# A decoder step on one core: a leeway behind the due time of the merge's and the group norm's matmuls, zero fills moved behind the first rows, and another order of lanes in a triangular solve

## The chip, the cores and the metric

The kernel runs on one core of a Trainium2 chip. The metric is the time of one execution on the device in microseconds. TensorE (PE in the profile) multiplies matrices, VectorE (DVE) and ScalarE (ACT) do elementwise work, GpSimd (POOL) helps with fills and some sums, and SyncE (SP) issues DMA transfers.

## What is computed

One layer of a decoder, for 2048 new tokens of one sequence and four tokens each of eight others, width 1024. Cut to what matters:

```python
h = _rmsnorm(x, norm_g)
p = jnp.einsum('bsd,dn->bsn', h, w_in)            # the large product
xin, bg, cg, zc = _split(p_conv, CONV_SIZES)      # short convolution branch
y_c = bg * conv * jax.nn.silu(zc)
...
def step(S, inp):                                 # RWKV-7 branch, 16 heads of 64
    r_t, k_t, v_t, d_t, kk_t, a_t = inp
    sa = jnp.einsum('bhvk,bhk->bhv', S, -kk_t)
    S = (S * d_t[:, :, None, :] + sa[..., None] * (kk_t * a_t)[:, :, None, :]
         + v_t[..., None] * k_t[:, :, None, :])
    y = jnp.einsum('bhvk,bhk->bhv', S, r_t)
    return S, y
...
mu = jnp.mean(ys, axis=-1, keepdims=True)         # group norm of each head
var = jnp.mean(jnp.square(ys - mu), axis=-1, keepdims=True)
yn = ((ys - mu) * lax.rsqrt(var + GN_EPS)).reshape(b, s, D_RWKV) * ln_w + ln_b
...
m = jax.nn.sigmoid(gc) * (y_c @ w_out_c) + jax.nn.sigmoid(gr) * (y_r @ w_out_r)
y = _rmsnorm(x + m @ w_o, final_g)
```

## The kernel before

**Main stream and side work.** TensorE executes its instructions in the order in which the program issues them. Most of them are the main stream: the projection of the normalised rows, held in two halves `XH` and `XL`, with the weights, also in two halves (`whl`), block by block of 128 columns, into PSUM tiles named `ip`. The 2048 tokens are taken in four sets of 512; the last set carries the 32 sample tokens too.

Between the matmuls of the main stream lies the recurrent branch, as side work. For each set and each of eight pairs of heads (32 pairs in all) it is cut into generators, called sides: `rwkv_keys` (kind "keys"), `rwkv_solve` ("solve"), `rwkv_merge` ("merge", L1260), `rwkv_load` ("load"), `rwkv_chain` ("chain", L1368), for the samples `rwkv_sequences` ("samp"), and `rwkv_out` ("out", L1483; for the very last pair it has the kind "close"). The recurrence is taken in chunks of 64 tokens. A chunk needs the inverse of a 64 by 64 triangular matrix; `rwkv_solve` inverts its 32 by 32 diagonal blocks row by row on VectorE, `rwkv_merge` puts the inverse together, and `rwkv_chain` then goes through the chunks with two kinds of matmul per chunk on the path, `pb<-UB,Xbd` and `pb<-SV,BKt`, behind `pa<-S,AR`.

**The planner.** While the program is built, a clock (`Clock`, L134 for `add`) follows every instruction with a cost from `cost` and notes when each result should be there. After every matmul of the main stream `drive` (L557) offers each live side a turn. `Side.run` takes a step of a side when its share of the window is due, when its VectorE backlog is small enough (not asked of the kinds listed in `URGENT`, among them chain, merge and load), and when the clock of TensorE has reached `self.due`. That due time is set by the step before: the side yields the operands that its next step needs, and L533 asks the clock when they are ready.

```python
self.due = clock.ready(aps) if aps else 0.0
```

So a product of a side is put into TensorE's order at the first main matmul behind the planned end of its operands. If an operand is late on the chip, TensorE waits with everything behind it. Each side may only begin when those named in its `after` list have ended: the chain of a pair behind the merge and the load of that pair and the "out" of the pair before (`run_pair`, L1781). When the ring of eight `tmp` buffers is empty, `push` (L543) forces steps of samples, keys and out without asking for the due time. The order of VectorE and ScalarE is that of the planned starts (`clock.begun`, near the end of the first phase); only the kinds listed in `LOOSE` are left out of it.

**The solve and the merge.** `rwkv_solve` turns `Mc` (32 rows of eight chunks) with one VectorE transpose of 1024 elements into `Mi`, so that a lane of 32 belongs to a chunk c and one of four column groups e; `X` starts as the identity `X0` in the same lane order. After 31 rows of updates a second transpose brings `X` back as `Xo` (it takes the buffer `Mi`, and stands in the trace as `Mi<-X`). `rwkv_merge` copies it on ScalarE in four copies to the block matrix `Xbd` (`Xbd<-Mi` in the trace), transposes a part on VectorE into `T11` (`Mc<-Xbd`), and yields; then come 16 small products `pt<-Mc,GM` and 16 `pt<-Mc,Mo`, two ScalarE copies, a yield, 32 products `pt<-Xbd,X`, copies, and a last yield. In the last set more products with the samples' part of `Xbd` follow, one step each. The planner's price of a VectorE transpose is 145 + 1.12 n ns up to 256 elements and 145 + 1.86 n ns above (L303); that of a ScalarE copy from SBUF is 190 + 0.84 n ns, and 190 + 1.9 n where the innermost stride of its input is over 1.

**The group norm.** `rwkv_out` subtracts the mean, squares on ScalarE, sums, takes the root (GpSimd's power and three VectorE steps), scales `Yc`, transposes it on TensorE (`pt<-ident,Yc`) and applies weights and gates. It yields operands four times.

**The start.** Two tiles of 128 rows of x are loaded into `GM`, their squares are summed on ScalarE, and `rsq_steps` (L595) gives the root: a VectorE `tensor_scalar`, the power on GpSimd, two products, a second `tensor_scalar` (`nw<-nw`) and a product (`rstd`). Then VectorE scales the first tile (`GM<-GM,rstd`, noted as `setup["scaled"][0]`) and ScalarE the second; TensorE transposes both in 16 pieces (`ip<-ident,GM`); VectorE, ScalarE and GpSimd split them into `XH` and `XL` (`to_cols`, L764); then the main stream begins. `zero_rest` (L1754) fills, on GpSimd, the buffers `UP`, `BK`, `AR`, `Xbd`, `UB`, `SV` and the eight states `S` with zeros. It stands later in the program, but its kind is in `LOOSE` and it depends on nothing, so the order of GpSimd has it wherever that engine has room.

After the last pair a second phase of some 590 us multiplies the branches with the output weights; the change does not touch it.

Every operation of the profile carries L264, the line of the helper that records it (`r = f(*a, **k)`), and every load and store of SyncE's queue L337.

Of the kernel before, what the change touches and what calls it, by code (L numbers as in the profile page):

```python
# [7 lines left out]
F32 = mybir.dt.float32  # L8
# [3 lines left out]
ALU = mybir.AluOpType  # L12
# [4 lines left out]
P = 128  # L17
# [4 lines left out]
NCH = 8  # L22
# [154 lines left out]


ROOM = {"samp": 2}


class Ring:
# [162 lines left out]
def hybrid_kernel(tc, x_prompt, x_sample, state_conv, state_shift, state_rwkv, norm_g, w_in, conv_w,  # L345
# [4 lines left out]
    clock = Clock()  # L350
    V, A, G, T = (Traced(e, n, clock) for e, n in ((nc.vector, "DVE"), (nc.scalar, "ACT"), (nc.gpsimd, "POOL"), (nc.tensor, "PE")))
# [15 lines left out]
    TW = NT + 64  # L367
# [37 lines left out]

    order = []
    raws, parts_, lows = {}, {}, []
    setup = {"casts": [], "lows": [], "scaled": {}}
    state = {"use": 0, "dma": 0, "split": 0}

    def w_advance(dma, split, load):
# [91 lines left out]
    class Side:  # L503
# [15 lines left out]
        def run(self, upto, force=False, once=False):  # L519
            if any(not x.ended for x in self.after) or upto < self.f0:  # L520
                return
            goal = float("inf") if once else weight[self.kind] * (upto - self.f0) / max(1e-9, self.f1 - self.f0) if upto < self.f1 else float("inf")
            while self.given < goal and self.f0 <= upto and (force or len(tmp.open) >= ROOM.get(self.kind, 0) and max(self.due, pt_free(self.banks)) <= clock.t["PE"] and (
                    self.kind in URGENT or clock.load("DVE") < BACKLOG)):
                try:
                    clock.kind = self.kind
                    x = next(self.g)
                    clock.kind = None
                    x, aps, self.banks = (x + ((), 0)[len(x) - 1:]) if isinstance(x, tuple) else (x, (), 0)
                    if x == "free":  # L530
                        self.f0, x = self.gate, 0.0
                    self.given += x
                    self.due = clock.ready(aps) if aps else 0.0  # L533
                    if once:
                        return
                except StopIteration:
                    clock.kind = None
                    weight[self.kind] = self.given
                    self.ended = True
                    live.remove(self)  # L540
                    break
# [68 lines left out]
    tmp = Ring(ph1.enter_context(tc.tile_pool(name="tmp", bufs=1)), [P, NT + 64], 8, clock)  # L610
# [62 lines left out]
    for hr in range(2):  # L673
        for q in range(2):
            sl = mask_p[hr * 64:(hr + 1) * 64, q]
            G.affine_select(out=sl, in_=sl, pattern=[[1, 64]], compare_op=ALU.is_gt if q == 0 else ALU.is_ge,
                            fill=0.0, base=0, channel_multiplier=-1)
# [3 lines left out]
    for hr in range(2):  # L681
        sl = seqm[hr * 64:(hr + 1) * 64, :]
# [9 lines left out]
                        in1=seqm.unsqueeze(2).broadcast_to([P, NS, SL]), op=ALU.mult)  # L692

    X0 = con.tile([P, 8, 32], F32, name="X0")
    xo0 = tmp.tile([P, TW], F32, name="tmp")[:, 0:256].rearrange("p (a b c) -> p a b c", b=4, c=8)
    G.memset(xo0, 1.0)
    for g in range(4):
        sl = xo0[g * 32:(g + 1) * 32]
        G.affine_select(out=sl, in_=sl, pattern=[[-4, 8], [-1, 4], [0, 8]], compare_op=ALU.is_equal, fill=0.0,
                        base=0, channel_multiplier=1)  # L700
    V.transpose(X0.rearrange("p a b -> p (a b)"), xo0.rearrange("p a b c -> p (a b c)"))
    tmp.free(xo0)

    rst = con.tile([P, NT], BF16, name="rst")
# [496 lines left out]
    col = [slice(32 * b, 32 * b + 32) for _ in range(2) for b in range(2)]  # L1201
    blk = [(slice(64 * h + 32 * b, 64 * h + 32 * b + 32)) for h in range(2) for b in range(2)]

    def rwkv_solve(th, p, o):

        AR = o["AR"]
        samp = th == LAST
        GM = GMB[(th * NB + p) % 2]


        yield 0.0, (), 2
        for c0 in range(0, NCH + samp, 4):
            cs = range(c0, min(NCH + samp, c0 + 4))
            pp = [new_pt([P, 512], F32, name="pt") for _ in range(2)]
            for c in cs:
                for h in range(2):
                    T.matmul(pp[h][:, (c - c0) * P:(c - c0 + 1) * P], lhsT=BK[HS[h], c].rearrange("p q t -> p (q t)"),
                             rhs=AR[HS[h], c].rearrange("p q t -> p (q t)"), start=True, stop=True)
            k = len(cs)
            mk = mask_s if c0 == NCH else mask_p  # L1220
            for h in range(2):
                V.tensor_tensor(out=GM[:, c0:c0 + k, :, h, :],
                                in0=pp[h][:, 0:k * P].rearrange("p (c a t) -> p c a t", a=2, t=64),
                                in1=mk.unsqueeze(1).broadcast_to([P, k, 2, 64]), op=ALU.mult)
            yield W["score"], (), 2 if c0 + 4 < NCH + samp else 0


        Mc = rw.tile([P, NCH, 32], F32, name="Mc")
        for i, g in enumerate(blk):
            h, b = i // 2, slice(i % 2 * 32, i % 2 * 32 + 32)  # L1230
            A.copy(Mc[g], GM[b, 0:NCH, 0, h, b])
        yield 0.5, [Mc]
        Mi = rw.tile([P, 32, 32], F32, name="Mi")
        V.transpose(Mi.rearrange("p t (e c) -> p t e c", c=NCH),
                    Mc.rearrange("p c t -> p t c").unsqueeze(2).broadcast_to([P, 32, 4, NCH]))
        X = rw.tile([P, 8, 32], F32, name="X")
        A.copy(X, X0)
        Mo = rw.tile([P, NCH, 32], F32, name="Mo")
        A.copy(Mo[64:96], GM[0:32, 0:NCH, 0, 1, 32:64])
        yield W["inv0"], [Mi, X]  # L1240

        for j in range(31, 0, -1):
            c0 = j // 4
            if c0 == 7:
                V.scalar_tensor_tensor(out=X[:, 7, 0:j], in0=Mi[:, j, 0:j], scalar=X[:, 7, j:j + 1], in1=X[:, 7, 0:j],
                                       op0=ALU.mult, op1=ALU.add)
                yield W["inv"]
                continue
            tt = sm.tile([P, 80], F32, name="tt")
            tv = tt[:, 0:(8 - c0) * j].rearrange("p (c i) -> p c i", i=j)  # L1250
            V.tensor_tensor(out=tv, in0=Mi[:, j, 0:j].unsqueeze(1).broadcast_to([P, 8 - c0, j]),
                            in1=X[:, c0:8, j:j + 1].broadcast_to([P, 8 - c0, j]), op=ALU.mult)
            V.tensor_tensor(out=X[:, c0:8, 0:j], in0=X[:, c0:8, 0:j], in1=tv, op=ALU.add)
            yield W["inv"]
        Xo = rw.tile([P, 32, 32], F32, name="Mi")[:, 0:8]
        V.transpose(Xo.rearrange("p c (a e) -> p a e c", e=4), X)
        o.update(GM=GM, Xo=Xo, Mo=Mo)
        yield W["inv"]

    def rwkv_merge(th, p, o):  # L1260

        GM, Xo, Mo = (o[k] for k in ("GM", "Xo", "Mo"))
        Xbd = o["Xbd"] = XB[(th * NB + p) % 2]
        samp = th == LAST
        for i, g in enumerate(blk):
            A.copy(Xbd[g, 0:NCH, col[i]], Xo[g])

        T11 = rw.tile([P, NCH, 32], F32, name="Mc")
        V.transpose(T11[0:96], Xbd[0:96, 0:NCH, col[0]])
# [476 lines left out]
    St = [xp.tile([P, P], F32, name=f"S{p}") for p in range(NB)]  # L1746
# [6 lines left out]
    scv = xp.tile([P, NB, 2 * NS], F32, name="scv")  # L1753
    def zero_rest():  # L1754
        for t in (UP[64:128, 1].bitcast(F32), UP[0:64, 3].bitcast(F32), BK[:, NCH], ARB[0][:, NCH], ARB[1][:, NCH], *XB, *UB, SV[:, NCH]):
            G.memset(t, 0.0)
        for p in range(NB):
            G.memset(St[p], 0.0)
        yield 1

    def end_(th, p):
# [5 lines left out]
    def begin_pair(th, p, total):  # L1767


        o = {}  # L1770
        k = th * NB + p
        f = [total * x for x in CUTS["end" if end_(th, p) else "most" if th < LAST else "last"]]
        def read(n):
            return [prior(x, n) for x in ("chain", "samp")]
        job["keys", k] = Side(rwkv_keys(th, p, o), "keys", [prior("load", k - 1), prior("solve", k - 1), prior("up", 0)] + read(k - 2)).over(0, f[3])
        job["solve", k] = Side(rwkv_solve(th, p, o), "solve", [job["keys", k], prior("merge", k - 1)] + read(k - 2)).over(f[3], f[4])
        job["merge", k] = Side(rwkv_merge(th, p, o), "merge", [job["solve", k]] + read(k - 2)).over(f[4], f[5])
        job["load", k] = Side(rwkv_load(th, p, o), "load", [job["keys", k]] + read(k - 1)).over(f[4], f[5])
        return o
# [17 lines left out]
    for th, hv, p, nx in plan:  # L1797
# [15 lines left out]
        e = EDGE / 2 * NB  # L1813
# [15 lines left out]
    SP.flush(0)  # L1829
    clock.planning = False  # L1830

    def behind_of(b, a):
        tc.add_manual_dep(b, a.name, mybir.DependencyInfo(
            mybir.DependencyClass.NoSync, mybir.DependencyReason.DATA), reason="keep_in_program_order")

    for ops in clock.begun.values():
        ops.sort(key=lambda o: o[0])
        for (_, a), (_, b) in zip(ops, ops[1:]):
            behind_of(b, a)
    for b in setup["lows"]:  # L1840
        behind_of(b, setup["scaled"][0])
    behind_of(setup["casts"][1], setup["scaled"][1])

    ph1.close()
# [372 lines left out]
```

## Time and profile before

| | |
|---|---|
| median of 3 runs | 3048.32 us (3045.91 to 3054.13) |
| the profiled execution's own time | 3047.81 us |
| its span, first to last instruction | 3046.1 us |
| TensorE's clock granted, mean over the span | 0.997 |
| busy: TensorE, VectorE, ScalarE, GpSimd | 2986.0, 2162.4, 1346.3, 316.0 us |

The profiled execution is 0.5 us below the median, and 1.7 us of its time lie outside the span. In a group's row the names are "out<-in" with buffer numbers left out; then come the shape, the count, the busy time, the mean duration of one in ns, and the idle time of that engine just before these instructions with what ended it. A busy TensorE is one with a matmul under way, and these overlap, so its waits are small gaps among many matmuls.

### The profile page before, as it was taken

How to read it: one execution, taken by the hardware profiler on the slowest of the kernel's cores; microseconds unless marked ns; L12 is line 12 of the kernel's file. 1: busy time of each engine (PE TensorE's matmuls, PEld its weight loads, DVE VectorE, ACT ScalarE, POOL GpSimd, SP SyncE). 2: the span in 40 equal slices, each digit the busy share in tenths (PEclk: the TensorE clock that was granted, in tenths of full speed). 3: DMA queues.
4: the chain of work that ended last, by engine and by line, in shares of the span. 5: the costliest groups of instructions: out<-in, count | busy, mean ns of one | idle time of the engine just before them, and what ended most of it. 6: DMA issues, size and time to landing. Idle time of an engine off the chain costs nothing. (4 is left out here: it accounts for less than half of the span.)

```text
span 3046.1 us, 56137 instructions
## 1 busy us (share of the span) xinstructions
PE 2986.0 (98%) x21370; PEld 2559.5 (84%) x21370; DVE 2162.4 (71%) x5504; ACT 1346.3 (44%) x2745; POOL 316.0 (10%) x520
## 2 busy tenths in 40 slices
PE   8999999999999999999999999999999999999998
PEld 6778777788888788788787899999999997888996
DVE  6777778767777777777777777667767744486575
ACT  4555555554444445444444444444444322324223
POOL 2011111011111111111111110000100000000000
PEclk9999999999999999999999999999999999999999
DMA  8877767766666667666666665444343588898775
GB/s 273 289 236 237 251 220 248 230 223 228 208 218 210 209 218 240 223 222 216 216 221 212 198 215 179 149 136 146 127 145 130 170 267 317 325 324 295 271 264 195
DMA packets 319731, 678.05 MB, mean 223 GB/s; under 512 B 47610, under 2 KB 179827, under 8 KB 269798
## 3 DMA queue, kind: packets, MB, share of 16 engines
q1 hardware_dynamic: 310758, 670.27, 64.9%
q10 hardware_dynamic: 8704, 4.20, 0.5%
q8 instruction: 169, 2.77, 0.4%
q14 instruction: 100, 0.82, 0.1%
HBM read 479.10 MB, written 195.28 MB: 221 GB/s over the span
## 5 line engine op out<-in xcount | busy, mean ns | idle before, releaser
L264 PE MATMUL ip<-XH,whl 128*128 128x512 f32 (+3 forms) x6832 | 1853.9, 351 | 5.8 <-DVE whl L264 3.8
L264 PEld LDWEIGHTS ip<-XH,whl 128*128 128x128 f32 x6832 | 1174.5, 189 | 137.1 <-DVE whl L264 6.8
L264 PE MATMUL ip<-XL,whl 128*128 128x512 f32 (+3 forms) x3416 | 1195.4, 350 | 0.0
L264 PEld LDWEIGHTS ip<-XL,whl 128*128 128x128 f32 x3416 | 646.8, 189 | 65.0 <-issue 5.5
L264 DVE SCALAR_TENSOR_TENSOR S<-pb,pe,sp 64x64 f32<-64x64 f32 x512 | 143.1, 279 | 98.1 <-PE pb L264 91.5
L264 DVE TENSOR_TENSOR X<-X,tt 128x60 f32<-128x60 f32 (+21 forms) x864 | 187.7, 217 | 27.9
L264 DVE TENSOR_TENSOR tt<-Mi,X 128x60 f32<-128x60 f32 (+21 forms) x864 | 188.9, 219 | 24.9
L264 ACT ACTIVATE sp<-S,pe 128x128 f32<-128x128 f32 x256 | 102.4, 400 | 205.6 <-DVE S L264 204.5
L264 ACT COPY SV<-pb 64x128 f32<-64x128 f32 x256 | 66.1, 258 | 283.8 <-PE pb L264 279.7
L264 DVE TENSOR_TENSOR UB<-pa,P 64x64 f32<-64x64 f32 x512 | 110.2, 215 | 109.9 <-PE pa L264 92.3
L264 ACT ACTIVATE tmp<-ip,vec 128x512 f32<-128x512 f32 (+2 forms) x174 | 103.0, 593 | 181.0 <-PE ip L264 175.7
L264 PE MATMUL acc<-XH,whl 128*128 128x264 f32 (+1 forms) x800 | 141.2, 329 | 0.5 <-DVE tmp L264 0.5
L264 PEld LDWEIGHTS acc<-XH,whl 128*128 128x128 f32 x800 | 119.0, 188 | 14.9 <-DVE tmp L264 0.7
L264 PE MATMUL acc<-UA,whl 128*128 128x264 f32 (+1 forms) x720 | 117.7, 324 | 1.9 <-DVE My L264 1.9
L264 PEld LDWEIGHTS pb<-UB,Xbd 128*128 128x128 f32 x512 | 85.0, 188 | 40.1 <-PE ip L264 15.5
L264 PEld LDWEIGHTS acc<-UA,whl 128*128 128x128 f32 x720 | 105.0, 190 | 13.4 <-DVE My L264 2.3
L264 DVE TENSOR_TENSOR whl<-wraw,whl 128x1024 fp32r<-128x1024 f32 x81 | 101.7, 1255 | 19.6 <-ACT whl L264 18.9
L264 DVE TENSOR_TENSOR GM<-pt,mask_p 128x512 f32<-128x512 f32 x128 | 82.6, 686 | 42.9 <-PE pt L264 42.5
L264 PE MATMUL pb<-UB,Xbd 128*128 128x128 f32 x512 | 105.0, 286 | 8.1 <-DVE UB L264 7.0
L264 PEld LDWEIGHTS pa<-S,AR 128*128 128x128 f32 x512 | 86.7, 188 | 26.3 <-DVE S L264 14.7
L264 PE MATMUL acc<-XL,whl 128*128 128x264 f32 (+1 forms) x616 | 108.6, 326 | 0.0
L264 PEld LDWEIGHTS pb<-SV,BKt 128*128 128x128 f32 x512 | 89.4, 188 | 20.6 <-ACT SV L264 6.5
(559 smaller groups left out, 4422.9 us busy)
## 6 DMA issues: line engine op xcount, KB each, us to landing
wraw<-in_w_in_dram SPq DMA_DIRECT2D x81, 512.0 KB
whl<-w_k SPq DMA_DIRECT2D x24, 1024.0 KB
whl<-w_r SPq DMA_DIRECT2D x24, 1024.0 KB
whl<-w_v SPq DMA_DIRECT2D x24, 1024.0 KB
whl<-w_z SPq DMA_DIRECT2D x24, 1024.0 KB
whl<-w_xin SPq DMA_DIRECT2D x24, 1024.0 KB
whl<-w_cg SPq DMA_DIRECT2D x24, 1024.0 KB
whl<-w_zc SPq DMA_DIRECT2D x24, 1024.0 KB
```

The costliest lines, as they stand in the source:

```text
L264: r = f(*a, **k)
```

## The change

Three edits. **Leeway:** for the kinds "merge" and "out" the due time is 1000 ns behind the planned time of the operands. **Fillings:** the memsets of `zero_rest` get a dependence on the first scaled tile; it is a real wait of GpSimd on VectorE (`Sync`), not only an order. **Lanes:** in the solve the lane order is (c, e) instead of (e, c): the four lanes of a chunk lie next to each other. The transpose into `Mi` then reads each element of `Mc` four times in a row, the transpose out of `X` writes without strides, and the four ScalarE copies to `Xbd` read runs of four elements instead of runs of 32.

```diff
+LEEWAY = {"merge": 1000.0, "out": 1000.0}
...
-                    self.due = clock.ready(aps) if aps else 0.0
+                    self.due = clock.ready(aps) + LEEWAY.get(self.kind, 0.0) if aps else 0.0
...
-    xo0 = tmp.tile([P, TW], F32, name="tmp")[:, 0:256].rearrange("p (a b c) -> p a b c", b=4, c=8)
+    xo0 = tmp.tile([P, TW], F32, name="tmp")[:, 0:256].rearrange("p (a c b) -> p a c b", b=4, c=8)
...
-        G.affine_select(out=sl, in_=sl, pattern=[[-4, 8], [-1, 4], [0, 8]], compare_op=ALU.is_equal, fill=0.0,
+        G.affine_select(out=sl, in_=sl, pattern=[[-4, 8], [0, 8], [-1, 4]], compare_op=ALU.is_equal, fill=0.0,
                         base=0, channel_multiplier=1)
...
-        V.transpose(Mi.rearrange("p t (e c) -> p t e c", c=NCH),
-                    Mc.rearrange("p c t -> p t c").unsqueeze(2).broadcast_to([P, 32, 4, NCH]))
+        V.transpose(Mi.rearrange("p t (c e) -> p t c e", c=NCH),
+                    Mc.rearrange("p c t -> p t c").unsqueeze(3).broadcast_to([P, 32, NCH, 4]))
...
-        V.transpose(Xo.rearrange("p c (a e) -> p a e c", e=4), X)
+        V.transpose(Xo.rearrange("p a b -> p (a b)"), X.rearrange("p a b -> p (a b)"))
...
         for i, g in enumerate(blk):
-            A.copy(Xbd[g, 0:NCH, col[i]], Xo[g])
+            A.copy(Xbd[g, 0:NCH, col[i]].rearrange("p c (a e) -> p c a e", e=4),
+                   Xo[g].rearrange("p a (c e) -> p c a e", e=4))
...
         for t in (UP[64:128, 1].bitcast(F32), UP[0:64, 3].bitcast(F32), BK[:, NCH], ARB[0][:, NCH], ARB[1][:, NCH], *XB, *UB, SV[:, NCH]):
-            G.memset(t, 0.0)
+            r = G.memset(t, 0.0)
+            setup["zeros"].append(r.ins)
         for p in range(NB):
-            G.memset(St[p], 0.0)
+            setup["zeros"].append(G.memset(St[p], 0.0).ins)
...
-    def behind_of(b, a):
-        tc.add_manual_dep(b, a.name, mybir.DependencyInfo(
-            mybir.DependencyClass.NoSync, mybir.DependencyReason.DATA), reason="keep_in_program_order")
+    def behind_of(b, a, kind=mybir.DependencyClass.NoSync):
+        tc.add_manual_dep(b, a.name, mybir.DependencyInfo(kind, mybir.DependencyReason.DATA), reason="keep_in_program_order")
...
+    for b in setup["zeros"]:
+        behind_of(b, setup["scaled"][0], mybir.DependencyClass.Sync)
```

More of the change, by code (lines that the diff above doesn't have):

```diff
@@ L407, in hybrid_kernel @@
     raws, parts_, lows = {}, {}, []
-    setup = {"casts": [], "lows": [], "scaled": {}}
+    setup = {"casts": [], "lows": [], "scaled": {}, "zeros": []}
     state = {"use": 0, "dma": 0, "split": 0}
@@ L698, in hybrid_kernel @@
         sl = xo0[g * 32:(g + 1) * 32]
-        G.affine_select(out=sl, in_=sl, pattern=[[-4, 8], [-1, 4], [0, 8]], compare_op=ALU.is_equal, fill=0.0,
+        G.affine_select(out=sl, in_=sl, pattern=[[-4, 8], [0, 8], [-1, 4]], compare_op=ALU.is_equal, fill=0.0,
                         base=0, channel_multiplier=1)
-    V.transpose(X0.rearrange("p a b -> p (a b)"), xo0.rearrange("p a b c -> p (a b c)"))
+    V.transpose(X0.rearrange("p a b -> p (a b)"), xo0.rearrange("p a c b -> p (a c b)"))
     tmp.free(xo0)
```

## The prediction

> **What bounds the kernel now.** I read the page first, then TensorE's waits, then the groups they stand before, then the timeline of the start and of two merges.
>
> ```profile
> PE 2986.0 (98%) x21370; PEld 2559.5 (84%) x21370; DVE 2162.4 (71%) x5504; ACT 1346.3 (44%) x2745; POOL 316.0 (10%) x520
> ```
>
> TensorE is busy for 2986.0 of 3046.1 us, and it takes its work in a fixed order. The change adds and removes no matmul, so it can only touch TensorE's waits: 60.1 us of idle, and matmuls that run slower than they could. The waits by cause (total us, times, longest us):
>
> ```profile
> PE ip L264 <- DVE GM L264: 11.2, 1, 11.2
> PE pt L264 <- DVE Mc L264: 7.3, 9, 2.1
> PE pb L264 <- DVE UB L264: 7.0, 17, 1.3
> ...
> PE pa L264 <- DVE S L264: 3.3, 8, 0.8
> ```
>
> The reader should see three places: one wait of 11.2 us at the start, the merge's wait for `Mc`, and the chain's own waits (UB and S: 7.0 + 3.3 = 10.3 us), which the change gives no leeway. The groups that do get a leeway (last column: idle before):
>
> ```profile
> L264 PE MATMUL pt<-Mc,GM 32*32 32x32 f32 x512 | 21.9, 192 | 7.8 <-DVE Mc L264 7.3 <-DVE nw L264 0.4
> L264 PE MATMUL pt<-Xbd,X 32*32 32x32 f32 x1024 | 22.7, 192 | 0.2 <-ACT SV L264 0.2
> L264 PE MATMUL pt<-ident,Xbd 128*128 128x128 f32 x8 | 2.4, 296 | 1.1 <-DVE Xbd L264 0.9 <-PE pt L264 0.2
> L264 PE MATMUL pt<-ident,Yc 128*128 128x128 f32 x136 | 20.3, 274 | 1.4 <-DVE Yc L264 1.2
> ```
>
> All idle time that a leeway for "merge" can remove is 7.8 + 0.2 + 1.1 = 9.1 us, and for "out" 1.4 us. That is the ceiling of that edit, but for the clock (below).
>
> **The fillings.** The timeline of the start (start, duration, engine):
>
> ```profile
> 8.84 0.16 DVE L264 TENSOR_TENSOR nw<-nw,nw 128x2 f32<-128x2 f32 x1
> 9.03 3.14 DVE L264 TENSOR_SCALAR nw<-nw 128x2 f32<-128x2 f32 x1
> ...
> 12.08 1.79 POOL L264 MEMSET S<- 128x128 f32 x8
> ...
> 12.40 1.33 DVE L264 TENSOR_SCALAR GM<-GM,rstd 128x1024 f32<-128x1024 f32 x1
> ...
> 13.65 1.20 DVE L264 TENSOR_TENSOR whl<-wraw,whl 128x1024 fp32r<-128x1024 f32 x1
> 13.79 3.67 PE L264 MATMUL ip<-ident,GM 128*128 128x128 f32 x16 [11.15 <-DVE GM L264]
> ...
> 18.09 1.27 POOL L264 TENSOR_TENSOR XL<-tmp,XH 128x512 fp32r<-128x512 f32 x1 [4.22 <-ACT XH L264]
> ...
> 22.55 0.17 DVE L264 TENSOR_SCALAR nw<-nw 128x2 f32<-128x2 f32 x1
> ...
> 22.96 0.75 DVE L264 TENSOR_SCALAR BKt<-BKt,rstd 128x1024 f32<-128x1024 f32 x1
> ```
>
> The same `nw<-nw` over 128x2 takes 3.14 us at 9.03, beside GpSimd's row of memsets, and 0.17 us at 22.55, when GpSimd fills nothing. The scaling of a tile takes 1.33 us beside the fills of `S` and 0.75 us at 22.96. The first transposes start 0.06 us behind that scaling (13.73). Without the fills in front, the path is shorter by (3.14 - 0.17) + (1.33 - 0.75) = 3.55 us. What is late next: GpSimd. The fills ran from 8.8 to 13.9; the last of them stretched while VectorE held `GM`. I count 3.3 us up to 12.08 and some 1.2 us for `S`, 4.5 us. They now begin when `GM` is scaled, at 13.73 - 3.55 = 10.2, and end near 14.7. Queued behind them is GpSimd's `XL<-tmp,XH`, whose operand would be there at 18.09 - 3.55 = 14.5, and TensorE's first `XL` matmuls need it. So 0.2 us are lost: 3.3 us remain. Bounds: 3.55 if GpSimd has this product in front of the fills, 0 if VectorE's next instruction, `whl<-wraw,whl`, is held until 14.7 as `nw<-nw` was. The row at 13.65 overlaps only the very end of the fills, with 1.20 us as elsewhere; the product at 8.84 (two inputs in SBUF) takes 0.16 us in front of the blocked instruction, beside the first fill. I take 3.3. The four `affine_select` of `X0` keep their element count; if the shorter inner run costs GpSimd something, it has 0.68 us of idle before the power of the root to hide it, and more than that would delay the start one for one.
>
> [...]
>
> **The lanes.** The groups of the two transposes and of the copies (busy us, mean ns):
>
> ```profile
> L264 DVE STREAM_TRANSPOSE Mi<-Mc 128x1024 f32<-128x1024 f32 x32 | 66.0, 2063 | 13.9 <-ACT Mc L264 13.6
> L264 DVE STREAM_TRANSPOSE Mi<-X 128x256 f32<-128x256 f32 x32 | 20.8, 650 | 0.9
> ```
> ```profile
> L264 ACT COPY Xbd<-Mi 32x256 f32<-32x256 f32 x128 | 51.7, 404 | 40.5 <-DVE Mi L264 38.9
> ```
>
> `Mi<-X` writes strided and takes 650 ns; the merge's other transpose, `Mc<-Xbd` (row in the next fence), has the same 256 elements a partition in runs of 32 and takes 440. The edit takes the strides away: 0.21 us less, on the path into the merge, and the planner's price (145 + 1.12 x 256 = 432 ns) becomes true. For `Mi<-Mc` the unstrided price, scaled from 440 at 256 elements, is at most 4 x 440 = 1760 ns and, with the 179 ns that a line through 650 and 2063 leaves at zero elements, 179 + 4 x 261 = 1220 ns. Its new reads are four equal ones in a row; I take 1300 (bounds 1220 to 2063). VectorE is spared 32 x (0.76 + 0.21) = 31 us, all of it off TensorE's path; it makes operands less late against a plan that still counts 2050 ns. ScalarE's copies read runs of four where they read runs of 32, and jump by more between them. I keep 404; the far bound is the planner's own price for strided input, 190 + 1.9 x 256 = 676 ns, four times 0.27 = 1.1 us later per merge.
>
> **The leeway.** One merge of the last set, all engines:
>
> ```profile
> 2330.32 0.66 DVE L264 STREAM_TRANSPOSE Mi<-X 128x256 f32<-128x256 f32 x1
> ...
> 2331.01 1.66 ACT L264 COPY Xbd<-Mi 32x256 f32<-32x256 f32 x4 [2.04 <-DVE Mi L264]
> ...
> 2332.28 0.44 DVE L264 STREAM_TRANSPOSE Mc<-Xbd 96x256 f32<-96x256 f32 x1 [0.56 <-ACT Xbd L264]
> ...
> 2332.78 0.21 PE L264 MATMUL pt<-Mc,GM 32*32 32x32 f32 x1 [0.71 <-DVE Mc L264]
> ```
>
> TensorE stood there 0.71 us before `Mc` was done: the plan had the operand that much too early. A due time 1.0 us later puts about four main matmuls in front, and the wait is gone. Of the nine waits for `Mc` (7.3 us) the longest, 2.1 us, leaves 0.9 behind 1.0 of leeway and 0.21 of transpose; the other eight share 5.2 us, 0.65 each, and one more may leave 0.5. The earlier `Mi` should halve these 1.4. I take 9.1 - 0.7 = 8.4 us for the merge, and 1.2 for out, where `Yc` accounts for 1.2 of the 1.4. The 2.1 us, in the first of these stretches, cost more than themselves (TensorE's busy time comes first, its clock third from the end):
>
> ```profile
> 644.30:647.70 3.40, 1.34 (x38) 1.13 (x38) 2.52 (x7) 2.57 (x6) 0.00 (x0) 1.00 0.66 275
> 647.70:651.10 3.40, 3.40 (x17) 3.32 (x18) 1.81 (x4) 2.03 (x5) 0.18 (x1) 0.51 0.24 31
> ```
>
> After a stretch with TensorE busy for 1.34 of 3.40 us, the granted clock is 0.51 for the next 3.4 us: another 1.7 us lost. With the wait at 0.9 us or less it should go.
>
> [...]
>
> What the leeway adds: a merge yields three operands (six in the last set), so it ends up to 3 us later (6 there), an "out" up to 4. Behind them waits the chain.
>
> ```profile
> 2336.10 0.74 ACT L264 COPY Xbd<-pt 32x256 f32<-32x256 f32 x2 [1.56 <-PE pt L264]
> ...
> 2343.35 0.59 ACT L264 COPY P<-pt 128x512 f32<-128x512 f32 x1 [1.80 <-PE pt L264]
> ```
>
> In this pair the chain's first copy comes 6.5 us behind the merge's last, so a slip of up to 6 us is covered. Where the cover is gone, the chain starts late and is placed more tightly, with more of its 10.3 us of waits. I charge 1.5 us (bounds -3, since VectorE is eased, to +8).
>
> **The sum:** 3.3 + 8.4 + 1.2 + 1.7 - 1.5 = 13.1 us less than the profiled 3047.8, so 3034.7; the median shown is 0.5 above that execution: 3035.
>
> **Rivals.** *The wait moves to the chain.* Leeway ends merges later and the chain's 10.3 us of waits double: 3035 + 10 = 3045. For it: TensorE's order is new from the first pair on; against: the 6.5 us above. *The fills hold VectorE later* (bound 0 of the start): 3038. *The leeway misses*, because operands slip with the steps that it delays: only the start and half of the rest, 3047.8 - 3.3 - 1.5 = 3043. *Slower: chains that catch up.* A chain that starts behind its window is placed step by step at its due times, 24 placed steps with a mean wait of 7.0 / 17 = 0.41 us: 9.9 us per pair. It cancels the gain from 13.1 / 9.9 = 1.3 pairs, and is slower by more than 9.1 us from 2.2 pairs on; three pairs give 3035 + 30 = 3065. It would be in the last set, where merges slip by six yields. Against it: the cover of 6.5 us, and 17 such waits in all now.
>
> **How the numbers follow.** Forecast 0.60; wait moves 0.16; fills hold VectorE 0.09; leeway misses 0.08; chains catch up 0.07. A measurement here tells about 0.3% (9.1 us) from no change, so faster means below 3039. Of the forecast 0.53 lies below that, of the fills' case 0.07: faster 0.60, same 0.33, slower 0.07. The bounds of the parts give for the forecast 3047.8 - (3.55 + 9.1 + 1.4 + 1.7 + 3) = 3029 at best and 3047.8 - (0 + 7 + 0.5 + 0) + 4 = 3044 at worst. The runs shown spread by 8 us, so I go to 3025 below, and to 3046 above to take in most of the moved wait.
>
> **What would show it.** Right: `nw<-nw` near 0.17 us and the first transposes near 10.2; fills of GpSimd from 10.2 on; `Mi<-X` at 0.44 us; idle before `pt<-Mc,GM` below 1.5 us; no stretch of half clock behind it. Wrong: UB and S waits well over 10.3 us together, `whl<-wraw,whl` held beside the fills, or `Xbd<-Mi` near 0.68 us.

## The result, and the profile after

| | before | after |
|---|---|---|
| median of 5 runs, same chip | 3048.32 us (3045.91 to 3054.13) | 3025.81 us (3023.29 to 3026.55) |
| the profiled execution | 3047.81 us | 3024.04 us |
| its span | 3046.1 us | 3022.3 us |

The ratio is 0.9923, with a 95% interval from 0.991 to 0.9937: faster by 22.5 us, where 13.3 were forecast. The median stands 0.8 us above the low end of the stated range (3025 to 3046); by the ratio, 0.9923 x 3048.32 = 3024.9, the time is just below it. Of all executions behind this document two, one of before (3218.83 us) and one of the leeway alone (4849.73 us), fell in a much slower state and are left out of the ratios. The page of after begins with the engines' busy times:

```profile
PE 2974.6 (98%) x21370; PEld 2556.4 (85%) x21370; DVE 2139.6 (71%) x5504; ACT 1341.8 (44%) x2745; POOL 322.0 (11%) x520
```

The instructions are as many as before, and TensorE's idle time, 3022.3 - 2974.6 = 47.7 us, is 12.4 us smaller. Its busy time fell by 11.4 us too, with the same matmuls: half of the gain lies where the column of idle time can't show it. Some 3.4 us of that half are granted clock: ahead of its end, before has three stretches of 3.4 us at half clock (0.51 granted from 647.7, 0.50 from 2026.7 and from 2555.8), after has one (0.51 from 429.1), and TensorE is busy throughout them (3.40 of 3.40 us), so that each costs 1.7 us. TensorE's waits in after (total us, times, longest us):

```profile
PE ip L265 <- DVE GM L265: 8.1, 1, 8.1
PE pb L265 <- DVE UB L265: 7.0, 12, 2.2
PE pb L265 <- ACT SV L265: 3.2, 6, 1.5
...
PE pt L265 <- DVE us L265: 2.6, 4, 1.2
...
PE ip L265 <- POOL XL L265: 2.2, 3, 1.2
PE pa L265 <- DVE S L265: 2.2, 5, 0.7
...
PE pt L265 <- DVE Mc L265: 1.2, 2, 0.9
```

The row of before for `Yc`, which is in no list above, was:

```profile
PE pt L264 <- DVE Yc L264: 2.5, 4, 1.2
```

`Mc` went from 7.3 to 1.2 us, `Yc` is gone from the list, and the start's wait is 3.1 us shorter. UB kept its 7.0 us but has a wait of 2.2 us, where 1.3 was the longest. The timeline of the start in after:

```profile
9.69 0.17 DVE L265 TENSOR_SCALAR nw<-nw 128x2 f32<-128x2 f32 x1
...
10.09 0.75 DVE L265 TENSOR_SCALAR GM<-GM,rstd 128x1024 f32<-128x1024 f32 x1
...
10.76 1.22 DVE L265 TENSOR_TENSOR whl<-wraw,whl 128x1024 fp32r<-128x1024 f32 x1
...
10.90 3.67 PE L265 MATMUL ip<-ident,GM 128*128 128x128 f32 x16 [8.07 <-DVE GM L265]
10.96 0.45 POOL L265 MEMSET UP<- 64x128 f32 x2 [1.56 <-DVE GM L265]
...
14.24 1.24 POOL L265 MEMSET S<- 128x128 f32 x8
...
15.44 1.27 POOL L265 TENSOR_TENSOR XL<-tmp,XH 128x512 fp32r<-128x512 f32 x1
...
15.82 0.77 PE L265 MATMUL ip<-XH,whl 128*128 128x256 f32 x2 [0.83 <-DVE tmp L265]
```

The fills stand behind the scaled tile, both VectorE steps have their short durations, and `whl<-wraw,whl` runs beside the fills in 1.22 us without being held. The first transposes start at 10.90 instead of 13.79, that is 2.89 us earlier. Last, the two transposes and the copies in after:

```profile
L265 ACT COPY Xbd<-Mi 32x256 f32<-32x256 f32 x128 | 51.6, 403 | 40.4 <-DVE Mi L265 38.5
L265 DVE STREAM_TRANSPOSE Mi<-Mc 128x1024 f32<-128x1024 f32 x32 | 39.8, 1243 | 18.1 <-ACT Mc L265 17.8
L265 DVE STREAM_TRANSPOSE Mi<-X 128x256 f32<-128x256 f32 x32 | 14.2, 444 | 0.9
```

Every duration came out as forecast (1300, 440, 404). So the prices of the instructions were right; what a shorter instruction is worth to TensorE was not.

### The profile page after: what moved, and what is told of

The parts are those of the page before. It is cut to its first block, busy times and chain, and to the rows that moved or that the text cites. A ratio compares the mean times of both kernels' runs of the same rounds, so it can differ in the third digit from the quotient of the medians.

```text
span 3022.3 us, 56107 instructions
## 1 busy us (share of the span) xinstructions
PE 2974.6 (98%) x21370; PEld 2556.4 (85%) x21370; DVE 2139.6 (71%) x5504; ACT 1341.8 (44%) x2745; POOL 322.0 (11%) x520
## 4 chain that ended last, share of the span: by engine, by line
PE 86%; DVE 8%; DMA 2%; ACT 2%; issue 1%; POOL 0%; SPq 0%; ACTq 0%; POOLq 0%; DVEq 0%
PE ip L265 53%; PE acc L265 16%; PE pt L265 11%; PE pb L265 4%; PE pa L265 2%; DVE tmp L265 2%; ACT tmp L265 1%; DVE whl L265 1%; DVE X L265 1%; DVE tt L265 1%; DMA wraw<-in_x_prompt_dram 1%; DVE S L265 1%; DVE sq L265 0%; DVE BK L265 0%; DVE cv L265 0%
```

## The experiments

Each of the kernels below ran 5 to 11 times beside before, which stood at medians of 3047.27 to 3048.25 us; a gain over before is counted from the before that ran beside the kernel, and a difference of two changed kernels is that of their medians.

### One edit at a time

```diff
# fills_only:  before + the dependence of the memsets on the scaled tile
# lanes_only:  before + the new lane order, both transposes, the copies
# leeway_only: before + LEEWAY = {"merge": 1000.0, "out": 1000.0}
# no_leeway:   after - LEEWAY (fillings and lanes)
```

> The kernel before with the fillings' edit alone; order of TensorE, VectorE and ScalarE as before. Theory A (the terms add: fillings 3, leeway 10 to 12, lanes the rest): 3 us less than before (ratio 0.999), first transposes near 10.5, everything later as before. Theory B (the undersized term is VectorE's relief by the lanes): the same here. Theory C (the start sets the phase of later waits, so that a shift of 3 us moves waits and half-clock stretches elsewhere): the total moves by something else than 3, up to 6 either way.

> The kernel before with the lanes' edit alone; all engines in the order of before. Theory A: waits for Mc fall by 0.2 us each plus what the earlier Mi gives, 3 to 4 us less than before in all. Theory B: VectorE runs 1 us per pair ahead of the plan, so half or more of the waits on VectorE go, not only the merge's: 8 to 12 us less, waits for Mc at 2 us or below of 7.3, waits for GM and Yc below before as well.

> The kernel before with the leeway alone; TensorE's order is that of the changed kernel, row by row. Theory A: 12 to 16 us less than before, waits for Mc near 2 us. Theory B: 6 to 9 us less, with the chain's and the score products' waits above those of the changed kernel. If the new order itself is what gives more than the leeway's waits, the waits outside merge and out fall here as they did in the changed kernel.

> The changed kernel without its leeway: fillings and lanes on the order of before. Theory A: 6 to 7 us less than before (3 from the start, 3 to 4 from the lanes). Theory B: 11 to 15 us less than before. The difference to the changed kernel is what the leeway is worth on top: 16 us by A, 8 to 11 by B.

| | us | ratio to before, 95% |
|---|---|---|
| fillings alone | 3041.84 | 0.998 (0.9971 to 0.9989) |
| lanes alone | 3033.44 | 0.9949 (0.9935 to 0.9963) |
| leeway alone | 3044.58 | 0.9988 (0.9979 to 0.9997) |
| fillings and lanes | 3031.3 | 0.9947 (0.9935 to 0.996) |
| all three | 3025.81 | 0.9923 (0.991 to 0.9937) |

The lanes, for which the prediction counted 0.7 us (the halved rest of the merge's waits), bring about 15 us, the fillings 6.4 in the medians, the leeway 3.7 alone and 5.5 on top of the two. The leeway alone did to its own waits what it was forecast to do. TensorE's waits in that kernel:

```profile
PE pb L265 <- DVE UB L265: 8.8, 14, 2.2
PE pa L265 <- DVE S L265: 3.6, 10, 0.7
...
PE pt L265 <- DVE us L265: 2.6, 4, 1.2
PE pt L265 <- DVE Mc L265: 2.5, 3, 1.8
...
PE ip L265 <- ACT whl L265: 1.2, 1, 1.2
PE ip L265 <- DVE BKt L265: 1.2, 1, 1.2
PE ip L265 <- POOL XL L265: 1.2, 3, 0.7
```

`Mc` fell by 4.8 us and `Yc` by 2.3 (its row, 0.2 us, stands further down), but UB and S rose by 2.1 together, `us` by 1.3, and `whl` from ScalarE, `BKt` and `XL`, with 1.2 us each, were not among the first rows of before. Most of what had been gained moved to the chain and its neighbours.

### Where the lanes' gain comes from

The kernel with the lanes alone has TensorE's order of before, row by row, but for some neighbouring small products inside a merge. So the two can be compared without any redrawing of the order: for each matmul the spacing, from the start of the matmul ahead to its own start, is taken in both traces, and the differences are added up by product. The same holds for the fillings alone, for fillings and lanes, and for xo_only and mi_only below; padded_before and price have orders of their own:

```diff
# xo_only: before, but the second transpose unstrided, and the copies write each float into another chunk
-        V.transpose(Xo.rearrange("p c (a e) -> p a e c", e=4), X)
+        V.transpose(Xo.rearrange("p a b -> p (a b)"), X.rearrange("p a b -> p (a b)"))
-            A.copy(Xbd[g, 0:NCH, col[i]], Xo[g])
+            A.copy(Xbd[g, 0:NCH, col[i]].rearrange("p c (a e) -> p a e c", e=4),
+                   Xo[g].rearrange("p a (e c) -> p a e c", e=4))
# mi_only: lanes_only, but the second transpose writes the order of before, and the copies are as before
+        V.transpose(Xo.rearrange("p c (a e) -> p a c e", e=4), X)
+            A.copy(Xbd[g, 0:NCH, col[i]], Xo[g])
# padded_before: before, and the plan is told 800 ns too much for the big transpose
+            if op == "transpose" and n > 256:
+                return 145 + 1.86 * n + 800
# price: after, and the plan is told what the transposes now take
-            per = {"transpose": 1.12 if n <= 256 else 1.86, ...
+            per = {"transpose": 1.07, ...
```

> The kernel before with the old lane order kept, so that the transpose into Mi stays slow (2.06 us), but with the transpose out of X written without strides (0.65 to 0.44 us) and the permutation put into the four ScalarE copies; TensorE's and VectorE's order is that of the lanes' edit. If the gain of the lanes comes from the 0.8 us of the transpose into Mi, which stands far from the merge: 0 to 4 us less than before, and the chain's waits for UB stay near 7 us. If it comes from the shorter path into the merge: 10 us or more, as with the lanes' edit, unless the ScalarE copies lose the 0.2 us again (each over 0.45 us).

> The kernel before with half of the lanes' edit: the big transpose Mi<-Mc in the new lane order, the second one (Mi<-X) still writes strided, ScalarE's copies contiguous as before. TensorE's order is that of before. Theory 'the path into the merge': the path is shorter by 0.82 us a merge instead of 1.02, so it keeps 0.8 of the 15 us that all lanes together gave: some 12 us less, 3033 to 3038, with waits for Mc, UB and S between those of before and of all lanes. Rival 'the last step alone': the big transpose stands far ahead of TensorE's operands and is hidden, all of the gain hangs on the transpose right before the copies: then within 3 us of before. Rival 'VectorE's spare time': 26 of 33 us spared, the same 12 us; it is told from the first by the row-by-row difference (waits elsewhere than behind merges would shrink too).

> The kernel before whose plan alone counts 0.8 us more for the transpose into Mi; the work is the same. If what the lanes give is the lead of the chip over the plan (the plan counts 2.05 us where 1.24 are taken), this gives a lead of 0.8 us too: 5 to 12 us less than before. If it is VectorE's own time that counts, nothing is gained: within 3 us of before.

> The changed kernel with the plan told the truth on transposes (1.24 us for Mi, 0.42 for the others), which takes the lead away. If the lead is what counts: slower than the changed kernel by 5 us or more, 3030 to 3038. If VectorE's own time counts: the same within 3 us, or a little faster as work can be placed more tightly.

| | us | ratio to before, 95% |
|---|---|---|
| xo_only | 3066.4 | 1.0068 (1.0055 to 1.008) |
| mi_only | 3032.32 | 0.9952 (0.994 to 0.9965) |
| padded_before | 3050.94 | 1.0017 (1.0008 to 1.0026) |
| price | 3043.93 | 0.999 (0.9981 to 0.9999) |

The groups in xo_only show that its trade went the wrong way:

```profile
L264 ACT COPY Xbd<-Mi 32x256 f32<-32x256 f32 x128 | 82.4, 644 | 35.7 <-DVE Mi L264 34.0
...
L264 PE MATMUL pt<-Mc,GM 32*32 32x32 f32 x512 | 22.2, 193 | 20.2 <-DVE Mc L264 17.8 <-ACT tmp L264 0.8 <-DVE nw L264 0.8
L264 DVE STREAM_TRANSPOSE Mi<-X 128x256 f32<-128x256 f32 x32 | 14.2, 444 | 0.9
```

VectorE is spared 0.2 us a merge, and the four copies take 0.24 us more each: the path into the merge is 0.76 us longer, and the kernel 19 us slower. Compared row by row with before, the spacing of TensorE's starts grew by 13.5 us in front of the first `pt<-Mc,GM` of the merges alone. So VectorE's spare time can't be the whole account: here it has more of it, and the kernel loses by the path into the merge.

In mi_only the second transpose wrote runs of four, not the strides I had expected, and took 445 ns; so this kernel is a second measurement of the same 1.02 us (0.82 and 0.2), at the same 15 us, a little more than the 12 that were expected of its half. It leaves open by its time what each of the two transposes is worth, and so the rival "the last step alone"; only the spacings speak on that. By its row-by-row difference to before (17.9 us between the two profiled executions), the largest shares are 5.5 us in front of the chain's `pb<-UB,Xbd`, 3.1 us at and behind the one wait for `My` in the second phase, and 3.3 us in front of the merge's first `pt<-Mc,GM`. (`My` is a tile of the second phase.) The other 6 us are spread over many products, 3.1 of them in front of the main stream's `ip<-XH,whl`, partly clock (mi_only has one stretch of half clock ahead of its end, before three; the mean granted clock is 0.999 against 0.997), and no run assigns the rest. Only 22 of 21,370 spacings changed by over 0.3 us, and these hold 4.5 of the 17.9 us.

Why should the chain gain, which the lanes do not touch? The timelines of before, VectorE and then TensorE, at one chunk of one pair:

```profile
1464.65 2.07 DVE L264 STREAM_TRANSPOSE Mi<-Mc 128x1024 f32<-128x1024 f32 x1
1466.64 0.56 DVE L264 SCALAR_TENSOR_TENSOR S<-pb,pe,sp 64x64 f32<-64x64 f32 x2
...
1470.88 0.45 DVE L264 TENSOR_TENSOR UB<-pa,P 64x64 f32<-64x64 f32 x2
```
```profile
1470.82 0.40 PE L264 MATMUL ip<-XL,whl 128*128 128x512 f32 x1
1471.05 0.39 PE L264 MATMUL ip<-XH,whl 128*128 128x512 f32 x1
1471.47 0.46 PE L264 MATMUL pb<-UB,Xbd 128*128 128x128 f32 x2
```

The same place in mi_only:

```profile
1455.98 1.25 DVE L264 STREAM_TRANSPOSE Mi<-Mc 128x1024 f32<-128x1024 f32 x1
1457.24 0.60 DVE L264 SCALAR_TENSOR_TENSOR S<-pb,pe,sp 64x64 f32<-64x64 f32 x2
...
1461.52 0.45 DVE L264 TENSOR_TENSOR UB<-pa,P 64x64 f32<-64x64 f32 x2
```
```profile
1462.13 0.40 PE L264 MATMUL ip<-XL,whl 128*128 128x512 f32 x1
1462.37 0.40 PE L264 MATMUL ip<-XH,whl 128*128 128x512 f32 x1
1462.60 0.39 PE L264 MATMUL pb<-UB,Xbd 128*128 128x128 f32 x2
```

VectorE has no pause between the big transpose and `UB`: the pair that solves shares the queue with the pair in its chain. In before `UB` starts 6.23 us behind the transpose's start, in mi_only 5.54 us. In before its product starts 0.42 us behind the main matmul ahead of it, where 0.23 is the pitch: 0.19 us are lost, yet the profile lists no wait, since the matmul ahead ends at 1471.05 + 0.39 = 1471.44 by its own row (the profile models these ends), only 0.03 us earlier. Sorted by their distance from the last `Mi<-Mc`, the 48 spacings in front of `pb<-UB,Xbd` that lie 2.5 to 10 us behind one hold 3.8 of the 5.5 us, the 80 at 10 to 40 us 1.6, and the other 384 together 0.04. In the kernel with the lanes alone it is 3.8 of 4.8 us. In xo_only, where the big transpose is as before, these 512 spacings change by 0.1 us, although its second transpose is the short one. So this share belongs to the big transpose.

The last two runs are about the plan. The changed kernel is built by a plan that still counts 2050 ns for a transpose of 1243. Told the new prices, the gain nearly goes: 3043.93, 18 us above after. But the same lead made in the plan, with the slow transpose, gives nothing in the one order that was run. Two waits of padded_before:

```profile
PE pb L264 <- DVE UB L264: 4.5, 10, 1.0
...
PE pt L264 <- DVE Mc L264: 2.7, 3, 2.1
```

They were 7.0 and 7.3 us in before, and still this kernel is 3.7 us slower. So neither "a lead over the plan" nor "a shorter path" explains all by itself; the lanes gave both at once. Where price loses can be read from its trace. The spacings in front of the chain's `pb<-UB,Xbd` and `pa<-S,AR` (512 of each in every kernel) add up to 193.6 us in after and 205.2 in price, 11.6 of the 18.1 us between the two profiled executions. With a general slack of 70 (next section) they are 189.8 and 202.8, 13.0 of 22.2 us. So most of the loss stands in front of the chain again.

### Is the leeway a gain or a draw of the order?

Any change of a cost places TensorE's order anew, and where it then falls looks like a draw. Ten kernels change only a number of the plan. `SLACK` is 60 ns that the plan adds to the time until a matmul's result can be read:

```diff
# leeway_900, leeway_1100, leeway_2000: after with another leeway
-LEEWAY = {"merge": 1000.0, "out": 1000.0}
+LEEWAY = {"merge": 900.0, "out": 900.0}
# merge_only
+LEEWAY = {"merge": 1000.0}
# slack50, slack70: no_leeway with another general slack; slack50_after, slack70_after,
# slack70_before, slack70_price: after, before and price with it
-SLACK = 60.0
+SLACK = 70.0
```

> The changed kernel with a leeway of 900 instead of 1000. Theory 'the waits that are named': a tenth of the leeway moves each merge by one half of a matmul at most; within 2 us of the changed kernel (3024 to 3028). Rival 'every new order is a draw': the order differs nearly everywhere, and the sum of small waits comes out anywhere within some 6 us: if it lies more than 3 us from 3025.8, a difference of the size that I had forecast for the leeway can't be told from a draw by one run of one value.

> The changed kernel with a leeway of 1100. Leeway by dose (1000 takes the waits away, 2000 gives back by the chain): within 2 us of 3025.8. A draw: from 3025 to 3034, as 900 with 3032.9 and 2000 with 3031.9.

> The changed kernel with a leeway of 2000 ns. If waits of the merge are what the leeway removes: the 1.2 us left for Mc go, a gain of 1 us at most, 3022 to 3026. If a later merge pushes the chain into tighter places: chain waits (UB, SV, S: 12.4 us in the changed kernel) up by 3 us or more and the time 3028 or above. A change of more than 5 us in either direction without either sign speaks for the order by itself.

> The changed kernel with the leeway for the merge alone. By my prediction's terms out's leeway is worth 1.2 us: 3027. If the leeway for out only costs (its waits were 1.4 us in all, and each out ends up to 4 us later): 3022 to 3025. Rival 'every new order is a draw': off by more than 3 us to either side.

> Fillings and lanes without the leeway (3031.3 before), the plan's general slack 70 instead of 60. Theory 'waits that are named': 10 ns a placed product, nothing that can be measured: 3029 to 3034. Rival 'every new order is a draw': anywhere from 3025 to 3037, and so tells how far kernels without a leeway scatter.

> Fillings and lanes, no leeway, slack 50. Third draw without a leeway (60 gave 3031.3, 70 gave 3029.3): 3026 to 3036 if the draws scatter as they did; waits for Mc between 2 and 6 us.

> The changed kernel with the plan's general slack at 70 instead of 60: the leeway on top of slack70 (3029.3 beside a before of 3047.4). If the leeway is worth the 5.5 us that separate the changed kernel from the one without it, under any neighbouring order: 3022 to 3026. If that difference was a draw of the order: anywhere from 3025 to 3034, as likely above 3029.3 as below.

> The changed kernel with slack 50, beside slack50. Leeway worth 5.5 us: 5 to 6 us below slack50. A draw: within 4 us of it on either side. Waits for Mc below 3 us in both cases.

> The kernel before with slack 70: a second order without lanes, fillings or leeway. If the 15 us of the lanes (with fillings 16 to 18) hold under any order, this lies 13 us or more above slack70 (3029.3): 3042 to 3052. If before was an unlucky order and the lanes only drew a better one: 3030 to 3038.

> The changed kernel with slack 70 and the plan told the transposes' measured prices (145 + 1.07 n); the changed kernel at slack 70 is at 3026.7, with these prices at slack 60 it was at 3043.9. If the lanes' worth is that operands come earlier than the plan counts, telling the plan takes the worth back: 3037 to 3046. If 3043.9 was an unlucky order: 3024 to 3034.

| general slack | 50 | 60 | 70 |
|---|---|---|---|
| before | | 3048.32 | 3047.2 |
| fillings and lanes, no leeway | 3031.25 | 3031.3 | 3029.27 |
| all three, leeway 1000 | 3040.76 | 3025.81 | 3026.71 |
| all three, plan told the new prices | | 3043.93 | 3044.18 |

| leeway at slack 60 | none | 900 | 1000 | 1100 | 2000 | 1000, merge alone |
|---|---|---|---|---|---|---|
| us | 3031.3 | 3032.86 | 3025.81 | 3028.76 | 3031.86 | 3027.51 |

The step of 17 to 18 us by fillings and lanes holds at slack 60 and 70, and so do the prices' 17 to 18. The leeway's does not: -5.5, -2.6 and +9.5 us at a slack of 60, 70 and 50, and at slack 60 between -5.5 and +1.6. Its ratios are 0.9973 (0.9963 to 0.9984) at slack 50 with it and 0.9944 (0.9931 to 0.9956) without. So 900 and 1000, where the expectation by named waits was a difference of 2 us at most, differ by 7, more than all that the leeway was worth at its best.

One collision that an order with a leeway can bring is easy to see. The timeline of after, around the 2.2 us of UB:

```profile
424.86 2.42 POOL L265 TENSOR_TENSOR rstd<-nw,mhalf 128x13 f32<-128x13 f32 x1 [3.61 <-DVE nw L265]
...
427.32 0.17 DVE L265 TENSOR_TENSOR nw<-rstd 128x13 f32<-128x13 f32 x1 [2.54 <-POOL rstd L265]
427.53 0.17 DVE L265 TENSOR_TENSOR nw<-nw,nw 128x13 f32<-128x13 f32 x1
427.74 0.17 DVE L265 TENSOR_SCALAR nw<-nw 128x13 f32<-128x13 f32 x1
427.82 0.21 DVE L265 TENSOR_TENSOR UB<-pa,P 64x64 f32<-64x64 f32 x1
...
428.51 0.46 PE L265 MATMUL pb<-UB,Xbd 128*128 128x128 f32 x2 [2.24 <-DVE UB L265]
```

VectorE stands 2.54 us before a norm's `nw<-rstd`, until GpSimd's power is done; the chain's `UB` is queued behind it, and TensorE behind that. The stretches that follow (TensorE's busy time first, its clock third from the end):

```profile
425.50:428.90 3.40, 1.16 (x7) 0.70 (x6) 1.45 (x7) 0.00 (x0) 1.78 (x1) 1.00 1.03 312
428.90:432.30 3.40, 3.40 (x11) 2.75 (x10) 0.81 (x3) 0.26 (x1) 0.00 (x0) 0.53 1.02 343
```

Here it costs 2.24 us and a stretch of half clock. The plan counts 1650 ns for such a power (L314), and this one took 2.42 us. The collision stands in after, in the leeway alone (2.25 us at 435.4), and in leeway_1100, slack50_after and price (1.8 to 2.25 us), with a half clock right behind it in after (0.53, the row above), the leeway alone and slack50_after only (mean granted clock 0.997 in these two executions, 0.998 in those of leeway_1100 and price); in none of before, fillings and lanes, slack50, slack70, leeway_900, merge_only and slack70_after did it hold TensorE for more than 1.4 us. So the leeway, in some orders, puts a chain's step just behind that norm. It doesn't explain the scatter: after has the collision and is the fastest of all, and leeway_900 is 7 us slower without it.

## Why the prediction was wrong

The sign was right and the size was not: 13.3 us forecast, 22.5 measured, at the very edge of the range. Two errors of opposite sign met, so that the time came nearer to the forecast than its terms did.

**The lanes: the step that failed.** "VectorE is spared 32 x (0.76 + 0.21) = 31 us, all of it off TensorE's path." The durations were right (1243 and 444 ns), "all of it off TensorE's path" was not. Fillings and lanes bring 17 to 18 us under two orders, where the sum has 3.3 for the fillings and 0.7 for the lanes; that an eased VectorE might help the chain stood there only as a bound, 3 us. Of the lanes' 15, in the comparisons row by row, some 5 us are chain products queued on VectorE behind the big transpose, and about 3 us the merge's own. The rest is not assigned. The leeway alone and after have one order, too: of the 20.7 us between their rows, 9.9 lie in front of UB and S, 3.0 at the start, 1.1 in front of `Mc`. I had looked at who waits for `Mi` and not at who stands behind it on its engine.

**The leeway: mis-sized.** 9.6 us were forecast, less 1.5 for the chain. The waits named did go (`Mc` 7.3 to 1.2 us, `Yc` to nothing, though the lanes alone already took `Mc` to 5.3). But what the leeway takes off them comes back elsewhere, the more in some orders: -5.5, -2.6 and +9.5 us at three settings. The rival "the wait moves to the chain" (3045) describes the leeway alone (3044.58, UB and S 10.3 to 12.4 us). That the full kernel still ran to 3025.81 is the doing of lanes and fillings, 18.8 us on the same order. Of the leeway's sum I can say only that its sign changes with a setting that should not matter; a mean effect of this size isn't shown.

**The ceiling.** "All idle time that a leeway for merge can remove is 9.1 us" read the idle column as the whole loss. Neighbouring main matmuls are 0.40 us long in the profile at a pitch of 0.23, so a wait of up to 0.17 us is no idle time. The idle time of UB is 7.0 us in before and 5.8 in mi_only; the spacings in front of it shrank by 5.5.

**The fillings: right.** 2.89 us at the first transposes and at the first main matmul (18.71 to 15.82), against 3.3. The difference to the 3.55 us of the two steps is that `nw<-nw` itself starts at 9.69 instead of 9.03. That is the lanes' doing, by a path that the prediction had named: the `affine_select` of `X0` with the shorter inner run. The last three of four, before and after:

```profile
5.17 2.04 POOL L264 TENSOR_SCALAR_AFFINE_SELECT tmp<-tmp 32x256 f32<-32x256 f32 x3
```
```profile
5.47 2.88 POOL L265 TENSOR_SCALAR_AFFINE_SELECT tmp<-tmp 32x256 f32<-32x256 f32 x3
```

All four together take 1.1 us more, GpSimd's 0.68 us of idle time hides only a part, and the power of the root begins at 8.54 instead of 7.88. In the fillings alone, with the old lanes, the first transposes start at 10.29, 3.5 us earlier than in before. As for the rest, GpSimd's `XL<-tmp,XH` does begin as the fills end (14.24 + 1.24 = 15.48). The 6.4 us of the medians of the fillings alone are more than that, but 3.4 us is just the near end of their interval (0.9971 to 0.9989). Between the two profiled executions the starts move by 3.2 us in all, 3.4 of it at the first transposes; a shorter wait for `My` without its half clock (2.8 us) is offset elsewhere, above all by a stretch of half clock of 6.8 us near 507 (the mean granted clock of that execution is 0.997).

**The clock: right in kind.** The 2.1 us wait and its half clock at 647 are gone, and another such pair came at 428; two more stretches of before, at 2026.7 and 2555.8, are gone too. Over the executions the mean granted clock was 0.9975 in 21 runs of before and 0.9984 in five of after; 0.0009 of 3046 us is 2.7 us of the 22.5, against 1.7 forecast. That a run may lack this term, the last 0 in the prediction's worst case, no run shows for the wait of 2.1 us; what the runs show is that the mean clock of one kernel differs from run to run (0.996 to 0.999 in 21 runs of before).

**The other rivals.** The fills did not hold VectorE later (`whl` beside them took 1.22 us). In before `nw<-nw` was held beside them (3.14 us against 0.17); no run shows what sets the two apart. Chains that catch up did not occur in after. Two numbers of the prediction don't follow from its words: "half of the rest" in "the leeway misses" would be 4.9 us and not 1.5, and the worst case adds 4 us where the chain's bound was 8. How far an order with a leeway can fall is shown by slack50_after (3040.76), with these waits of the chain:

```profile
PE pb L265 <- DVE UB L265: 5.8, 11, 2.3
...
PE pa L265 <- DVE S L265: 3.4, 8, 1.1
PE pb L265 <- ACT SV L265: 3.2, 3, 2.6
```

Here, too, the sum of idle time (12.4 us, as in after: 7.0 + 3.2 + 2.2) doesn't show the 15 us between the two. In the profiled executions (17.2 us apart) some 5 us are clock, four stretches of 3.4 us at half clock against one (mean granted clock 0.997 against 0.999), and 6.7 us lie in the spacings in front of `pb<-UB,Xbd` and `pa<-S,AR` (200.3 us in all, 193.6 in after).

**Open.** Why the plan with true prices is 17 to 18 us slower at two settings, most of it in front of the chain, while a lead given by the plan alone is worth nothing in the one order tried. A margin between the plan and the chip, without later due times, fits both, but no run took that margin away in another way, and the order of TensorE differs in each of these pairs.

Three changes of the access order changed a duration: four equal reads in a row (1243 against 2063 ns), writes in runs of four floats (445 against 650), and ScalarE's writes that put each float into another chunk (644 against 404). Why they do is not shown by any run.

## What to carry to other kernels

When an instruction on a side engine gets shorter, list what stands behind it in that engine's queue, not only what waits for its result: here the largest share that could be assigned, about a third, stood in front of another pair's steps. Before a placing rule is credited with a few us, place the same kernel a few times with a setting that should not matter; if the results scatter as widely as the gain, it can't be told from the luck of one order. Where matmuls overlap, compare the spacing of starts under the same order, since the idle column hides every wait shorter than the tail of the matmul ahead (0.17 us here: 0.40 us long at a pitch of 0.23).

## What the runs showed of the hardware

A VectorE transpose of 128x256 written in runs of four floats takes 445 ns, the same as without strides (444), and 650 when each float lands apart; ScalarE's copy takes as long reading runs of four as reading 256 in a row (403 and 404), and 644 when it writes each float into another chunk, 128 floats on. GpSimd's `affine_select` over 32x256 went from 0.64 to 0.92 us with an inner run of four instead of eight. VectorE's product of two SBUF tiles was not slowed beside GpSimd's memsets (1.22 us in after, and 1.21 in before at 15.55, without them), while the `tensor_scalar` `nw<-nw` was held (3.14 us beside them in before, 0.17 in after without them). Stretches of half clock inside a run were 3.4 us long in before and after (0.50 to 0.51 granted) and 6.8 us in the fillings alone, behind the wait of 1.71 us for `Mc` at 504.9 (mean granted clock of that execution 0.997). Before has the same order and the same wait there, 1.71 us at 508.4, and no half clock behind it (1.00 granted from 508.4 to 515.2): whether a wait costs clock as well is not fixed by its length.
